# Two layers on one core: four instead of three groups of feed-forward columns by Strassen's product, second factors made in two portions, and another rule for the buffers of the condition sums

## The chip, the cores and the metric

The kernel runs on one core of a Trainium2 chip. The metric is the device time of one execution in microseconds (us). Three runs of the kernel before took 1845.4, 1853.11 and 1854.9, median 1853.11. The engines are named as in the profile: PE multiplies matrices (PEld is its loading of weights), DVE is VectorE, ACT is ScalarE, POOL is GpSimd, SP is SyncE; SP issues most loads.

## The reference

Two equal layers work on x of 512 tokens by 1024 features, in float32. A vector of conditions, `c_act = silu(c)`, gives six vectors of 1024 per layer:

```
mod = c_act @ w_ada + b_ada
shift1, scale1, gate1, shift2, scale2, gate2 = split(mod, 6)
h = rms_norm(x, norm1_g) * (1 + scale1) + shift1
...                                  # h @ w_in, three mixers (retention, gated linear, attention)
x = x + gate1 * (sum(gates * y_br) @ w_o)
h2 = rms_norm(x, norm2_g) * (1 + scale2) + shift2
u, g = split(h2 @ w_up, 2)           # 2 x 2816 columns
u = causal_dwconv(u, w_conv, b_conv) # three taps along the tokens
x = x + gate2 * ((silu(u) * g) @ w_down)
```

The change touches three places: the products `h2 @ w_up`, the sums `c_act @ w_ada` (the *condition sums*), and the pace at which the latter are put into the program.

## The kernel before, in words

Activations lie with features on the 128 partitions and the 512 tokens along the free dimension. A float32 product is made of three products of rounded parts (`mm3`, L320): high weight by high activation, high by low, low by high. All weights lie in DRAM as *units* of 128 x 1024 (512 KB), 338 of them, in the order of use. SP loads a unit into one of six raw buffers (`wr`, L180); ACT rounds it to its high part `wh` (L194); DVE takes `wl = wr - wh` (L203); then the raw buffer is free. A unit feeds 24 matmuls (8 blocks of 128 x 128, three products each). Weights are prepared some units ahead of their use: `depth` is how many units are rounded ahead, `far` how many more loads are issued.

The order of every engine's instructions is the order in which the Python program writes them; each engine goes through its own in order. `tick()` is called every few matmuls and puts in the next pieces of side work.

*Condition sums.* There are 80 blocks of `w_ada`, each 512 KB, which are summed beside the other work (another 32 half blocks are done at the start). One `ada_step` sums the block that was loaded in the step before (L230: a multiplication by `cact` and the sum along the free dimension) and then issues the next block's load (`ar`, L225) on SP. The block goes into one of the six raw buffers. `buffer()` takes the buffer that has been free longest, by `held`, which names for each the unit that used it last; the sum writes `held[ada_buf[0]] = -1`. A step is made in every second tick while `ada_on` is set, and in every tick while `ada_fast` is set. `ada_need(l, sec)` makes all steps up to a given sixth of the vector at once. Of the 80 sums, 34 stand in layer 0's merge and output product, 15 in its feed-forward product, 26 in its down product, and 5 in layer 1's merge.

*The feed-forward product* has 22 blocks of 128 columns for u and as many for g; a plain block takes two units (one of u, one of g), in 48 matmuls of 512 tokens, and `ff_evac` (L1072 and the lines before: scale, two taps, silu, product by g). The first three blocks stand with the normalization. Blocks 3 to J0 - 1 are plain, and the rest goes in groups of four by Strassen's product in Winograd's form: tokens are halved, the 1024 rows and the columns of a pair of blocks are halved, and 7 products replace 8. A group of four blocks takes 14 units where plain blocks take 8, with matmuls of 256 tokens (L1159, L1161, L1162). The combinations of the weights are made by loads that add to what is in the raw buffer (`accum_op`, on POOL's queue, L186, 8 per group). The combinations of the second factor, h2, are four sums per k (`ta`, `tb`; each holds two side by side) and their high and low parts (`tah`, `tal`, `tbh`, `tbl`), made once per layer for k = 0 to 3 and used by all groups: `t_sum` (5 DVE and 3 ACT operations) and `t_low` (3 DVE operations), one of these eight pieces after each of the first eight plain units. Within a group the evacuations are put at fixed units through `due`.

*The down product* has 8 blocks of 128 features over 22 k: the first three together, then one at a time; layer 0's last block is made by token halves, with the next layer's normalization behind it.

Of the kernel before, what the change touches and what calls it, by code (L numbers as in the profile page):

```python
# [50 lines left out]
NC = _o  # L51


NG = 3
J0 = KFF - 4 * NG
NI = 3
DN = [(j, k) for k in range(KFF) for j in range(NI)] + [(j, k) for j in range(NI, KD) for k in range(KFF)]
# [34 lines left out]
def tile_hybrid_layers(ctx: ExitStack, tc: tile.TileContext, xT, cvec, wall, wada, par, a2, cst, tabs, out):  # L92
# [23 lines left out]
    def free(n=1):  # L116
        live[0] -= n
# [108 lines left out]
            ada_raw.append((l, b, post, r))  # L226

    def ada_sum(l, b, r):
        held[ada_buf[0]] = -1
        V.scalar_tensor_tensor(out=r, in0=r, scalar=1.0, in1=cact, op0=ALU.mult, op1=ALU.mult,  # L230
                               accum_out=mod[l][:, b:b + 1])

# [59 lines left out]
    def tick(n=1, fl=True):  # L292
        for g in active:
            g[2] = False
        if cool[0] > 0:
            cool[0] -= 1
        if queue and len(active) < 8 and cool[0] == 0:
            it, cool[0] = queue.pop(0)
            active.append([it, next(it), False])
        advance("e")  # L300
        if fl:
            flush()
        advance("p")
        if ada_on[0] and (ada_fast[0] or tickcount[0] % 2 == 1):
            ada_step()
        tickcount[0] += 1
        if DBG:
            print("T", tickcount[0], len(active), len(queue), live[0], cur[0], [g[0].__name__ for g in active])
# [1 line left out]
    tickcount = [0]  # L310
    cool = [0]
    ada_on = [True]
    ada_fast = [False]

    def drain():
        flush()
# [249 lines left out]
    def layer(l, nm, h):  # L566
# [526 lines left out]

        tmid = {}

        def t_sum(k):
            ta, tb = slot("ta"), slot("tb")
            c, d = tks.pop((l, k)), tks.pop((l, k + 4))
            V.tensor_tensor(ta[:, H0], c[:, H0], c[:, H1], op=ALU.subtract)
            V.scalar_tensor_tensor(out=ta[:, H1], in0=d[:, H1], scalar=-1.0, in1=ta[:, H0], op0=ALU.mult,  # L1100
                                   op1=ALU.subtract)
            V.scalar_tensor_tensor(out=tb[:, H0], in0=d[:, H1], scalar=tabd[:, k:k + 1], in1=c[:, H1], op0=ALU.add,
                                   op1=ALU.subtract)
            V.tensor_tensor(tb[:, H1], d[:, H1], d[:, H0], op=ALU.subtract)
            V.tensor_tensor(tb[:, H1], tb[:, H1], ta[:, H0], op=ALU.add)
            ah, bh = slot("tah", F32R), slot("tbh", F32R)
            A.copy(ah[:, H0], ta[:, H0])
            A.activation(ah[:, H1], ta[:, H1], AF.Identity, bias=tabd[:, 4 + k:5 + k])
            A.copy(bh, tb)
            tmid[k] = ta, tb, ah, bh  # L1110

        def t_low(k):
            ta, tb, ah, bh = tmid.pop(k)
            al, bl = slot("tal", F32R), slot("tbl", F32R)
            V.tensor_tensor(al[:, H0], ta[:, H0], ah[:, H0].bitcast(F32), op=ALU.subtract)
            V.scalar_tensor_tensor(out=al[:, H1], in0=ta[:, H1], scalar=tabd[:, 4 + k:5 + k],
                                   in1=ah[:, H1].bitcast(F32), op0=ALU.add, op1=ALU.subtract)
            V.tensor_tensor(bl, tb, bh.bitcast(F32), op=ALU.subtract)
            tt[k, 1], tt[k, 2] = (ah, al, 0), (ah, al, 256)
            tt[k, 3], tt[k, 4] = (bh, bl, 0), (bh, bl, 256)  # L1120

        TS = [lambda: t_sum(0), lambda: t_low(0), lambda: t_sum(1), lambda: t_low(1),
              lambda: t_sum(2), lambda: t_low(2), lambda: t_sum(3), lambda: t_low(3)]

        def ff_group(j0):
            flush()
# [73 lines left out]
            def gate(t, i):  # L1200
                j = j0 + 2 * t + i
                V.tensor_tensor(act[j], act[j], gg[t][:, col(t, i)], op=ALU.mult)

            for t in range(2):
                at(1 + t, e1, t)
                at(3 + t, e5, t)
# [28 lines left out]
        ahead()  # L1235
        for j in range(3):
            pend.append(lambda j=j: ff_evac(j, fb[2 * j], fb[2 * j + 1]))
        free(NA)
        far[0] = 6
        for j in range(3, J0):  # L1240
            hold = {}

            def pu_evac(o, hold=hold):
                hold["u"] = o

            def pg_evac(o, hold=hold, j=j):
                ff_evac(j, hold["u"], o)

            col_block(h2, pu_evac)
            if TS:  # L1250
                TS.pop(0)()
            col_block(h2, pg_evac)
            if TS:
                TS.pop(0)()
        ada_on[0] = False
        far[0] = 12
        while ada_raw:
            i, b, post, r = ada_raw.pop(0)
            ada_sum(i, b, r)
            if post:  # L1260
                post()
        flush()
        for g in range(NG):
            ff_group(J0 + 4 * g)
# [33 lines left out]
                square_acc(j, acc3)  # L1298

        xl = list(range(KD))  # L1300
        act_to(4)
        far[0] = 4
        o2 = [bm() for _ in range(NI)]
        for kc in range(KFF):
# [9 lines left out]
                x[k] = slot("x")  # L1314
                Q.dma_start(out=x[k], in_=xm[l, k])
            if kc == 8:
                ada_on[0] = True
                ada_fast[0] = True
                far[0] = 1
            if kc % 2:  # L1320
                tick()
        ada_need(l, 5)
        for j in range(NI):
            pend.append(lambda j=j: dn_evac(j, o2[j]))
        for j in range(NI, KD if last else KD - 1):
            o = bm()
            for kc in range(KFF):
                wh, wl = wd(j, kc)
                mm3(o, wh, wl, acts[kc][0], acts[kc][1], kc == 0, kc == KFF - 1)
                if kc % 4 == 3:  # L1330
                    tick()

            pend.append(lambda j=j, o=o: dn_evac(j, o))
        flush()
        ada_fast[0] = False
        if last:
            return None, None
        ada_need(l + 1, 0)
# [218 lines left out]
```

## Time and profile before

| | |
|---|---|
| median of 3 runs | 1853.11 us |
| the profiled execution | 1846.68 us, span 1844.5 us |
| PE busy | 1784.8 us (97%) |
| DVE busy | 1085.7 us (59%) |
| ACT busy | 743.5 us (40%) |
| granted PE clock, mean | 0.985 |
| loaded from DRAM | 250.00 MB, 140 GB/s over the span |

The profile is one execution. A window of the trace (`A:B`, from the span's start) gives for each engine its busy time and the number of its instructions, then the granted PE clock, the share of time in which the load engines were busy, and the rate. A row of the timeline has start, duration, engine, line, operation, output <- inputs; in brackets stand the idle time before it and what ended that. A row of the waits has who waited for what: total us, how often, the longest. A costliest-groups row has count, busy us and mean ns, then the idle time just before. Lines are those of the kernel before. PE's matmuls overlap, so their pace is read from the distance of their starts, and a PE that is "busy" all the time may still run at half clock.

### The profile page before, as it was taken

Reading aid. Unit: us, or ns where it says so; the run is one execution under the profiler, and the core shown is the slowest. Engines: PE = TensorE matmul, PEld = TensorE weight load, DVE = VectorE, ACT = ScalarE, POOL = GpSimd, SP = SyncE. Lnnn points to the kernel's source line nnn. Section 1 sums busy time; section 2 is a strip of 40 time slices with the busy share of each in tenths; the row PEclk is TensorE's granted clock in tenths of the full one; section 3 lists DMA queues with packets and bytes.
Section 4 is the critical chain, followed back from the end, with each engine's and each line's share of the span. In section 5 each row is a group of like instructions: output and inputs, shape, how many; then the busy total and the mean of one; then the engine's idle time right before and its main releaser. Section 6 shows DMA issues by size and latency. Waiting matters only on the chain.

```text
span 1844.5 us, 24358 instructions
## 1 busy us (share of the span) xinstructions
PE 1784.8 (97%) x9601; PEld 1527.7 (83%) x9601; DVE 1085.7 (59%) x1639; ACT 743.5 (40%) x1233; POOL 147.7 (8%) x191
## 2 busy tenths in 40 slices
PE   8999999999899979999869999999999999999999
PEld 6888788888788869998668888788888898899887
DVE  7767654555566766685445667554434466566831
ACT  4664433422234335562115744333323234455520
POOL 3211100000010011100000101000000000111000
PEclk9999999999999989999979999999999999999999
DMA  9331232454462468854453322314242333488421
GB/s 359 126 130 58 74 99 83 146 181 177 168 223 97 161 184 215 212 200 166 177 194 110 108 92 69 104 69 149 92 147 93 122 108 92 121 210 217 160 99 50
DMA packets 78510, 259.99 MB, mean 141 GB/s; under 512 B 9096, under 2 KB 9522, under 8 KB 78396
## 3 DMA queue, kind: packets, MB, share of 16 engines
q1 hardware_dynamic: 68748, 224.86, 34.9%
q0 software_dynamic: 9648, 33.58, 8.6%
q8 instruction: 75, 1.23, 0.3%
q14 instruction: 39, 0.32, 0.0%
HBM read 250.00 MB, written 8.40 MB: 140 GB/s over the span
## 4 chain that ended last, share of the span: by engine, by line
PE 72%; DVE 12%; DMA 8%; ACT 4%; issue 3%; SPq 0%; POOL 0%; DVEq 0%; ACTq 0%; POOLq 0%
PE bm L321 13%; PE bm L322 13%; PE bm L323 13%; DMA ar<-wada 6%; PE bm L460 4%; PE ga L460 4%; PE bm L628 3%; PE bm L629 3%; PE bm L630 3%; PE bm L1159 3%; PE bm L1162 3%; PE bm L1161 3%; DMA wr<-wall 3%; DVE ar L230 2%; DVE wl L203 2%
## 5 line engine op out<-in xcount | busy, mean ns | idle before, releaser
L203 DVE TENSOR_TENSOR wl<-wr,wh 128x1024 fp32r<-128x1024 f32 x338 | 412.4, 1223 | 291.2 <-ACT wh L194 288.1
L194 ACT CAST wh<-wr 128x1024 fp32r<-128x1024 f32 x338 | 351.5, 1047 | 363.2 <-DMA wr<-wall 210.6
L321 PE MATMUL bm<-hhi,wh 128*128 128x512 f32 x912 | 366.1, 401 | 0.0
L323 PE MATMUL bm<-hhi,wl 128*128 128x512 f32 x912 | 355.7, 390 | 0.0
L322 PE MATMUL bm<-hlo,wh 128*128 128x512 f32 x912 | 355.5, 390 | 0.0
L321 PEld LDWEIGHTS bm<-hhi,wh 128*128 128x128 f32 x912 | 171.3, 188 | 37.1 <-issue 2.8
L323 PEld LDWEIGHTS bm<-hhi,wl 128*128 128x128 f32 x912 | 171.2, 188 | 37.1
L322 PEld LDWEIGHTS bm<-hlo,wh 128*128 128x128 f32 x912 | 171.5, 188 | 35.8 <-issue 1.4
L323 PE MATMUL bm<-fah,wl 128*128 128x512 f32 (+1 forms) x374 | 145.9, 390 | 17.2 <-DVE wl L203 17.2
L230 DVE SCALAR_TENSOR_TENSOR ar<-ar,cact 128x1024 f32<-128x1024 f32 x80 | 97.8, 1222 | 91.9 <-DMA ar<-wada 91.8
L321 PE MATMUL bm<-fah,wh 128*128 128x512 f32 (+1 forms) x374 | 145.7, 390 | 1.1 <-ACT wh L194 1.1
L322 PE MATMUL bm<-fal,wh 128*128 128x512 f32 (+1 forms) x374 | 144.9, 387 | 0.0
L323 PEld LDWEIGHTS bm<-fah,wl 128*128 128x128 f32 x374 | 74.5, 199 | 31.9 <-DVE wl L203 18.8
L628 PE MATMUL bm<-wh,hhi 128*128 128x512 f32 (+1 forms) x256 | 96.1, 376 | 0.0
L629 PE MATMUL bm<-wl,hhi 128*128 128x512 f32 (+1 forms) x256 | 93.5, 365 | 0.0
L630 PE MATMUL bm<-wh,hlo 128*128 128x512 f32 (+1 forms) x256 | 93.3, 365 | 0.0
L321 PEld LDWEIGHTS bm<-fah,wh 128*128 128x128 f32 x374 | 74.6, 200 | 14.3 <-ACT wh L194 1.4
L322 PEld LDWEIGHTS bm<-fal,wh 128*128 128x128 f32 x374 | 74.5, 199 | 13.1
L186 POOL DMA_DIRECT2D wr<-wall x48 | 41.7, 987 | 377.3 <-DVE wl L203 215.2
L321 PE MATMUL bm<-mxh,wh 128*128 128x256 f32 (+1 forms) x176 | 59.8, 340 | 8.0 <-ACT mxh L562 8.0
L322 PE MATMUL bm<-mxl,wh 128*128 128x256 f32 (+1 forms) x176 | 59.6, 338 | 0.0
L323 PE MATMUL bm<-mxh,wl 128*128 128x256 f32 (+1 forms) x176 | 59.1, 336 | 0.0
(288 smaller groups left out, 3368.5 us busy)
## 6 DMA issues: line engine op xcount, KB each, us to landing
wr<-wall SPq DMA_DIRECT2D x302, 512.0 KB, 4.3
ar<-wada SPq DMA_DIRECT2D x80, 512.0 KB, 3.5
wr<-wall POOLq DMA_DIRECT2D x48, 512.0 KB, 9.2
ad<-wada SPq DMA_DIRECT2D x32, 256.0 KB, 6.4
x<-xT SPq DMA_DIRECT2D x16, 256.0 KB, 4.5
x<-xm SPq DMA_DIRECT2D x16, 256.0 KB, 5.9
xm<-x POOLq DMA_DIRECT2D x10, 256.0 KB, 2.5
cumb<-cumd POOLq DMA_DIRECT2D x8, 256.0 KB, 4.8
```

Source lines behind the costliest of these rows:

```text
L194: A.copy(hi, raw[plan[i][1]])
L203: V.tensor_tensor(lo, raw[plan[i][1]], hi.bitcast(F32), op=ALU.subtract)
L230: V.scalar_tensor_tensor(out=r, in0=r, scalar=1.0, in1=cact, op0=ALU.mult, op1=ALU.mult, accum_out=mod[l][:, b:b + 1])
L321: T.matmul(o, lhsT=wh, rhs=ah, start=first, stop=False)
L322: T.matmul(o, lhsT=wh, rhs=al, start=False, stop=False)
L323: T.matmul(o, lhsT=wl, rhs=ah, start=False, stop=last)
L460: T.matmul(banks[f % GB][:, ts], lhsT=got[f // 8][wi][:, (f % 8) * 128:(f % 8) * 128 + 128], rhs=h[kc][hi][:, ts], start=kc == 0 and hf != ...
L628: T.matmul(o, lhsT=h[k][0][:, bs], rhs=wh[:, ws], start=k == 0, stop=False)
L629: T.matmul(o, lhsT=h[k][0][:, bs], rhs=wl[:, ws], start=False, stop=False)
L630: T.matmul(o, lhsT=h[k][1][:, bs], rhs=wh[:, ws], start=False, stop=k == KD - 1)
L1159: T.matmul(o, lhsT=wh[:, sl], rhs=ah, start=first and i == 0 and k == 0, stop=False, skip_group_check=True)
L1161: T.matmul(o, lhsT=wh[:, sl], rhs=al, start=False, stop=False, skip_group_check=True)
```

## The change

A group more per layer goes by Strassen's product: NG is 4, so J0 is 6; three plain blocks (6 units) remain behind the first three and 16 of the 22 blocks (56 units) are in groups. The second factor's combinations are cut into 16 pieces (`ta_sum`, `ta_low`, `tb_sum`, `tb_low` for k = 0 to 3). Twelve of them, the ta ones first, stand two after each of the six plain units; the other four (`TL`) stand in the first group, one at each of its units 1 to 4. The buffer of a condition sum is marked as freed by the newest unit (`state["lo"] - 1`), so it is taken last. The condition sums stop ahead of the plain blocks (the one that is still open is summed there) and start again when the first three down blocks are through, a step in every second tick; in the later down blocks a tick comes every three k, no longer every four. `ada_fast` goes. Of the 80 sums, 34 stand in layer 0's merge and output product as before, one ahead of its plain blocks, 13 in its down product and 32 in layer 1's merge and output product.

```diff
-NG = 3
+NG = 4
...
     def ada_sum(l, b, r):
-        held[ada_buf[0]] = -1
+        held[ada_buf[0]] = state["lo"] - 1
...
-        if ada_on[0] and (ada_fast[0] or tickcount[0] % 2 == 1):
+        if ada_on[0] and tickcount[0] % 2 == 1:
             ada_step()
...
-    ada_fast = [False]
...
-        def t_sum(k):
-            ta, tb = slot("ta"), slot("tb")
-            c, d = tks.pop((l, k)), tks.pop((l, k + 4))
+        def ta_sum(k):
+            ta, ah = slot("ta"), slot("tah", F32R)
+            c, d = tks[l, k], tks[l, k + 4]
             V.tensor_tensor(ta[:, H0], c[:, H0], c[:, H1], op=ALU.subtract)
             V.scalar_tensor_tensor(out=ta[:, H1], in0=d[:, H1], scalar=-1.0, in1=ta[:, H0], op0=ALU.mult,
                                    op1=ALU.subtract)
+            A.copy(ah[:, H0], ta[:, H0])
+            A.activation(ah[:, H1], ta[:, H1], AF.Identity, bias=tabd[:, 4 + k:5 + k])
+            tmid[k] = ta, ah
+
+        def ta_low(k):
+            ta, ah = tmid[k]
+            al = slot("tal", F32R)
+            V.tensor_tensor(al[:, H0], ta[:, H0], ah[:, H0].bitcast(F32), op=ALU.subtract)
+            V.scalar_tensor_tensor(out=al[:, H1], in0=ta[:, H1], scalar=tabd[:, 4 + k:5 + k],
+                                   in1=ah[:, H1].bitcast(F32), op0=ALU.add, op1=ALU.subtract)
+            tt[k, 1], tt[k, 2] = (ah, al, 0), (ah, al, 256)
+
+        def tb_sum(k):
+            tb, bh = slot("tb"), slot("tbh", F32R)
+            ta, _ = tmid[k]
+            c, d = tks.pop((l, k)), tks.pop((l, k + 4))
             V.scalar_tensor_tensor(out=tb[:, H0], in0=d[:, H1], scalar=tabd[:, k:k + 1], in1=c[:, H1], op0=ALU.add,
                                    op1=ALU.subtract)
             V.tensor_tensor(tb[:, H1], d[:, H1], d[:, H0], op=ALU.subtract)
             V.tensor_tensor(tb[:, H1], tb[:, H1], ta[:, H0], op=ALU.add)
-            ah, bh = slot("tah", F32R), slot("tbh", F32R)
-            A.copy(ah[:, H0], ta[:, H0])
-            A.activation(ah[:, H1], ta[:, H1], AF.Identity, bias=tabd[:, 4 + k:5 + k])
             A.copy(bh, tb)
-            tmid[k] = ta, tb, ah, bh
-
-        def t_low(k):
-            ta, tb, ah, bh = tmid.pop(k)
-            al, bl = slot("tal", F32R), slot("tbl", F32R)
-            V.tensor_tensor(al[:, H0], ta[:, H0], ah[:, H0].bitcast(F32), op=ALU.subtract)
-            V.scalar_tensor_tensor(out=al[:, H1], in0=ta[:, H1], scalar=tabd[:, 4 + k:5 + k],
-                                   in1=ah[:, H1].bitcast(F32), op0=ALU.add, op1=ALU.subtract)
+            tmid[k] = tb, bh
+
+        def tb_low(k):
+            tb, bh = tmid.pop(k)
+            bl = slot("tbl", F32R)
             V.tensor_tensor(bl, tb, bh.bitcast(F32), op=ALU.subtract)
-            tt[k, 1], tt[k, 2] = (ah, al, 0), (ah, al, 256)
             tt[k, 3], tt[k, 4] = (bh, bl, 0), (bh, bl, 256)
 
-        TS = [lambda: t_sum(0), lambda: t_low(0), lambda: t_sum(1), lambda: t_low(1),
-              lambda: t_sum(2), lambda: t_low(2), lambda: t_sum(3), lambda: t_low(3)]
+        TS = [lambda k=k, f=f: f(k) for k, f in ((0, ta_sum), (1, ta_sum), (0, ta_low), (2, ta_sum), (1, ta_low),
+                                                 (3, ta_sum), (2, ta_low), (0, tb_sum), (3, ta_low), (1, tb_sum),
+                                                 (0, tb_low), (2, tb_sum))]
+        TL = [lambda k=k, f=f: f(k) for k, f in ((1, tb_low), (3, tb_sum), (2, tb_low), (3, tb_low))]
...
+            for n in range(len(TL)):
+                at(1 + n, TL.pop(0))
             for t in range(2):
...
-        free(NA)
-        far[0] = 6
-        for j in range(3, J0):
-            hold = {}
-
-            def pu_evac(o, hold=hold):
-                hold["u"] = o
-
-            def pg_evac(o, hold=hold, j=j):
-                ff_evac(j, hold["u"], o)
-
-            col_block(h2, pu_evac)
-            if TS:
-                TS.pop(0)()
-            col_block(h2, pg_evac)
-            if TS:
-                TS.pop(0)()
         ada_on[0] = False
-        far[0] = 12
         while ada_raw:
             i, b, post, r = ada_raw.pop(0)
             ada_sum(i, b, r)
             if post:
                 post()
+        free(NA)
+        far[0] = 6
+        for j in range(3, J0):
+            hold = {}
+
+            def pu_evac(o, hold=hold):
+                hold["u"] = o
+
+            def pg_evac(o, hold=hold, j=j):
+                ff_evac(j, hold["u"], o)
+
+            col_block(h2, pu_evac)
+            for _ in range(2):
+                TS.pop(0)()
+            col_block(h2, pg_evac)
+            for _ in range(2):
+                TS.pop(0)()
+        far[0] = 12
         flush()
         for g in range(NG):
             ff_group(J0 + 4 * g)
...
         xl = list(range(KD))
+        ada_need(l, 5)
         act_to(4)
...
             if kc == 8:
-                ada_on[0] = True
-                ada_fast[0] = True
                 far[0] = 1
             if kc % 2:
                 tick()
-        ada_need(l, 5)
+        ada_on[0] = True
...
-                if kc % 4 == 3:
+                if kc % 3 == 2:
                     tick()
```

DVE in layer 0's down product, before: L230 is a condition sum, L203 a weight's low part, L1023 and L361 the evacuation of an output block.

```order
L203 TENSOR_TENSOR wl<-wr,wh 128x1024
L230 SCALAR_TENSOR_TENSOR ar,mod_88<-ar,cact 128x1024 x2
L203 TENSOR_TENSOR wl<-wr,wh 128x1024
L230 SCALAR_TENSOR_TENSOR ar,mod_88<-ar,cact 128x1024 x2
L203 TENSOR_TENSOR wl<-wr,wh 128x1024
L1023 SCALAR_TENSOR_TENSOR x<-bm,mod_87,x 128x512
L361 TENSOR_TENSOR acc<-acc,sq 128x512
L230 SCALAR_TENSOR_TENSOR ar,mod_88<-ar,cact 128x1024 x2
L203 TENSOR_TENSOR wl<-wr,wh 128x1024
```

The same place now; the evacuation's lines are L1022 and L360 in the new file.

```order
L203 TENSOR_TENSOR wl<-wr,wh 128x1024
L230 SCALAR_TENSOR_TENSOR ar,mod_88<-ar,cact 128x1024
L203 TENSOR_TENSOR wl<-wr,wh 128x1024
L230 SCALAR_TENSOR_TENSOR ar,mod_88<-ar,cact 128x1024 x2
L203 TENSOR_TENSOR wl<-wr,wh 128x1024
L1022 SCALAR_TENSOR_TENSOR x<-bm,mod_87,x 128x512
L360 TENSOR_TENSOR acc<-acc,sq 128x512
L230 SCALAR_TENSOR_TENSOR ar,mod_88<-ar,cact 128x1024
L203 TENSOR_TENSOR wl<-wr,wh 128x1024
L230 SCALAR_TENSOR_TENSOR ar,mod_88<-ar,cact 128x1024
```

Before, two sums stand between every weight and the next; now one and two in turn.

DVE at the start of layer 1's plain blocks, before: L1099 to L1105 are `t_sum`, L1115 to L1118 `t_low`, L1066 to L1078 a block's evacuation.

```order
L1099 TENSOR_TENSOR ta<-ht 128x256
L1100 SCALAR_TENSOR_TENSOR ta<-ht,ta 128x256
L1102 SCALAR_TENSOR_TENSOR tb<-ht,tabd 128x256
L1104 TENSOR_TENSOR tb<-ht 128x256
L1105 TENSOR_TENSOR tb<-tb,ta 128x256
L203 TENSOR_TENSOR wl<-wr,wh 128x1024
L1115 TENSOR_TENSOR tal<-ta,tah 128x256
L1116 SCALAR_TENSOR_TENSOR tal<-ta,tabd,tah 128x256
L1118 TENSOR_TENSOR tbl<-tb,tbh 128x512
L203 TENSOR_TENSOR wl<-wr,wh 128x1024
L1066 SCALAR_TENSOR_TENSOR fu<-bm,par_86,fu 128x511
L1068 SCALAR_TENSOR_TENSOR fu<-bm,par_86,fu 128x510
```

The same place now: L1098 and L1099 are `ta_sum`, L1108 and L1109 `ta_low`, L1065 to L1077 the evacuation.

```order
L1098 TENSOR_TENSOR ta<-ht 128x256
L1099 SCALAR_TENSOR_TENSOR ta<-ht,ta 128x256
L1098 TENSOR_TENSOR ta<-ht 128x256
L1099 SCALAR_TENSOR_TENSOR ta<-ht,ta 128x256
L203 TENSOR_TENSOR wl<-wr,wh 128x1024
L1108 TENSOR_TENSOR tal<-ta,tah 128x256
L1109 SCALAR_TENSOR_TENSOR tal<-ta,tabd,tah 128x256
L1098 TENSOR_TENSOR ta<-ht 128x256
L1099 SCALAR_TENSOR_TENSOR ta<-ht,ta 128x256
L203 TENSOR_TENSOR wl<-wr,wh 128x1024
L1065 SCALAR_TENSOR_TENSOR fu<-bm,par_86,fu 128x511
L1067 SCALAR_TENSOR_TENSOR fu<-bm,par_86,fu 128x510
```

The tb sums have moved behind all four ta sums. The weights' low parts keep their places, with two pieces between one and the next. The next rows of the same engine reach the low part that the first group's fourth unit uses (L203, the last row); L1117 to L1120 are `tb_sum`, L1127 is `tb_low`.

```order
L1117 SCALAR_TENSOR_TENSOR tb<-ht,tabd 128x256
L1119 TENSOR_TENSOR tb<-ht 128x256
L1120 TENSOR_TENSOR tb<-tb,ta 128x256
L203 TENSOR_TENSOR wl<-wr,wh 128x1024
L1127 TENSOR_TENSOR tbl<-tb,tbh 128x512
L1117 SCALAR_TENSOR_TENSOR tb<-ht,tabd 128x256
L1119 TENSOR_TENSOR tb<-ht 128x256
L1120 TENSOR_TENSOR tb<-tb,ta 128x256
L1065 SCALAR_TENSOR_TENSOR fu<-bm,par_86,fu 128x511
L1067 SCALAR_TENSOR_TENSOR fu<-bm,par_86,fu 128x510
L1077 TENSOR_TENSOR fu<-fu,bm 128x512
L203 TENSOR_TENSOR wl<-wr,wh 128x1024
```

Before, the last of the combinations stood behind the eighth of 14 plain units; now two `tb` sums and a `tb` low part stand within the two weights ahead of this one.

More of the change, by code (lines that the diff above doesn't have):

```diff
@@ L1237, in layer @@
             pend.append(lambda j=j: ff_evac(j, fb[2 * j], fb[2 * j + 1]))
+        ada_on[0] = False
+        while ada_raw:
+            i, b, post, r = ada_raw.pop(0)
+            ada_sum(i, b, r)
+            if post:
+                post()
         free(NA)
@@ L1249, in layer @@
             col_block(h2, pu_evac)
-            if TS:
+            for _ in range(2):
                 TS.pop(0)()
             col_block(h2, pg_evac)
-            if TS:
+            for _ in range(2):
                 TS.pop(0)()
-        ada_on[0] = False
         far[0] = 12
[L1257 to L1261, printed above, removed]
         flush()
@@ L1334, in layer @@
         flush()
-        ada_fast[0] = False
         if last:
```

## The prediction

> **What bounds the kernel now.** I read the busy shares first, then the chain that ended last.
>
> ```profile
> PE 1784.8 (97%) x9601; PEld 1527.7 (83%) x9601; DVE 1085.7 (59%) x1639; ACT 743.5 (40%) x1233; POOL 147.7 (8%) x191
> PE 72%; DVE 12%; DMA 8%; ACT 4%; issue 3%; SPq 0%; POOL 0%; DVEq 0%; ACTq 0%; POOLq 0%
> ```
>
> PE is nearly always at work, but the chain runs through it for only 72% of the time; for 20% the end was set by VectorE and by loads. To see where, I cut the span into stages that exist in both layers, with the same matmuls in each, and put the layers beside each other.
>
> ```profile
> core 0: us, PE busy (x) PEld busy (x) DVE busy (x) ACT busy (x) POOL busy (x), PEclk, DMA share, GB/s
> 62.82:589.34 526.52, 516.41 (x2652) 431.27 (x2651) 318.30 (x504) 213.86 (x407) 39.19 (x42) 0.99 0.38 132
> 1009.30:1523.34 514.04, 511.91 (x2650) 429.41 (x2649) 281.36 (x437) 207.34 (x397) 38.97 (x42) 1.00 0.31 104
> 589.34:665.50 76.16, 76.16 (x338) 63.06 (x336) 55.88 (x91) 29.38 (x41) 1.84 (x2) 1.00 0.49 159
> 1523.34:1599.49 76.15, 76.15 (x337) 63.06 (x336) 48.97 (x74) 33.44 (x47) 2.65 (x3) 1.00 0.33 94
> 665.50:805.11 139.61, 125.70 (x1010) 124.63 (x1008) 92.20 (x109) 72.61 (x94) 19.15 (x22) 0.95 0.78 200
> 1599.49:1720.45 120.96, 120.96 (x1010) 120.95 (x1008) 81.42 (x92) 68.92 (x89) 18.06 (x21) 1.00 0.81 205
> 805.11:963.33 158.22, 134.15 (x605) 113.43 (x603) 85.59 (x125) 39.11 (x54) 5.10 (x9) 0.90 0.52 186
> 1720.45:1840.15 119.70, 119.70 (x530) 98.92 (x528) 45.62 (x54) 31.59 (x42) 0.00 (x0) 1.00 0.27 95
> ```
>
> In pairs, layer 0 then layer 1: projections with merge and output product; the 14 plain feed-forward units; the 42 Strassen units; the down product. Layer 1's PE never waits after the merge (busy equals length, granted clock 1.00). Layer 0 is 12.5, 0, 18.65 and 38.5 us longer. What layer 0 has and layer 1 nearly lacks is the condition sums (75 of their 80). Their rows:
>
> ```profile
> L230 DVE SCALAR_TENSOR_TENSOR ar<-ar,cact 128x1024 f32<-128x1024 f32 x80 | 97.8, 1222 | 91.9 <-DMA ar<-wada 91.8
> ar<-wada SPq DMA_DIRECT2D x80, 512.0 KB, 3.5
> SPq L225 <- DVE ar L230: 402.5, 66, 24.8
> 859.77 1.23 DVE L230 SCALAR_TENSOR_TENSOR ar<-ar,cact 128x1024 f32<-128x1024 f32 x1 [2.14 <-DMA ar<-wada]
> 864.55 1.23 DVE L230 SCALAR_TENSOR_TENSOR ar<-ar,cact 128x1024 f32<-128x1024 f32 x1 [3.55 <-DMA ar<-wada]
> ```
>
> The sums' work is small (97.8 us); their wait for their own loads is as long (91.8 us). The third row is the sync queue: 66 of the loads waited for the sum before, 402.5 us in all, and in that time the weight loads queued behind them did not start. The reason is `held[...] = -1`: the buffer just summed counts as the one free longest, so the next load goes into it and can't start before the sum. One step is then load 3.5 plus sum 1.2, about 4.8 us (859.77 to 864.55), in VectorE's order. In the down product a step comes every four matmul triples once the first three columns are done. A matmul's spacing there:
>
> ```profile
> 1589.97 0.39 PE L321 MATMUL bm<-hhi,wh 128*128 128x512 f32 x1
> 1590.20 0.39 PE L322 MATMUL bm<-hlo,wh 128*128 128x512 f32 x1
> ```
>
> 0.227 us (finer over a whole unit: 76.15 / 14 = 5.44 per unit of 24), so four triples are 2.7 us against a step of 4.8: PE waits for VectorE.
>
> **The change, part by part.** The sum goes against the profiled execution's 1846.7 us (span 1844.5 and 2.2 around it); the median of the runs is 1853.1.
>
> *Condition sums in layer 0's down product: -36.* The stage is 158.22 against 119.70; 2.5 of that stays, by my estimate: layer 0's last column is made by halves (for the output product's last column, which is cut alike, that costs 18.15 in place of 3 x 5.44 = 16.3) and it carries the next layer's squares.
>
> ```profile
> 536.48:554.63 18.15, 18.15 (x154) 18.15 (x152) 9.18 (x21) 4.72 (x10) 3.71 (x7) 1.00 0.66 238
> ```
>
> So 36.0 is stall. After the change 13 sums run here in place of 26, one every six triples (4.1 us), and each load goes to a buffer freed four to seven VectorE operations ago, by the order, so it starts early. If it were serial all the same, 13 steps would each lose 4.8 - 4.1 = 0.7, some 10 us: the term lies between -26 and -36. I take -36, since 13 sums with 22 units are 35 loads of 0.52 MB in 122 us, 150 GB/s, and the Strassen stage moves 205 without a wait.
>
> *Layer 0's Strassen stage: -18.65.* Its first wait stands at its head:
>
> ```profile
> 684.87 0.58 PE L1159 MATMUL ba<-tah,wh 128*128 128x256 f32 x1 [9.14 <-ACT wh L194]
> ```
>
> Weights were late because SP's queue stood behind condition loads up to the stage's head, and one of the six buffers was theirs. Now the sums are off before the plain blocks, so all six serve weights. What is late next there is the second term below.
>
> *Layer 0's merge: -12.5* (526.52 - 514.04). Most of it is one wait:
>
> ```profile
> 509.11 0.79 PE L321 MATMUL bm<-mxh,wh 128*128 128x512 f32 x1 [7.27 <-ACT mxh L562]
> ```
>
> The same 34 sums stay in this stage; only their waiting goes. VectorE's 318.30 of 526.52 us leaves room for them.
>
> *Layer 1's merge gets 32 sums in place of 5: 0.* They are 27 x 1.22 = 33 us on a VectorE busy 281.36 of 514.04, and bring the stage to layer 0's load of 318. The end to the bad is the 12.5 that layer 0 loses with the same sums and the old buffer rule.
>
> *A fourth group by Strassen's product in each layer: -6.4.* Eight plain units become 14 units of 256-wide matmuls:
>
> ```profile
> 1649.89 0.28 PE L1159 MATMUL ba<-tah,wh 128*128 128x256 f32 x1
> 1650.01 0.28 PE L1161 MATMUL ba<-tal,wh 128*128 128x256 f32 x1
> ```
>
> A unit is 120.96 / 42 = 2.88, a group 14 x 2.88 = 40.3 against 8 x 5.44 = 43.5: -3.2 per layer. The Trainium skill, "TensorE: Matmul & The Clock Gate", section "Back-to-back issue gap", speaks against the change: it gives a stream of matmuls about 81 ns apart at width 128 and 131 ns at 512. Interpolated to 98 at 256 (an estimate from that page), a group would be 24 x 14 x 0.098 = 32.9 against 24 x 8 x 0.131 = 25.2, a loss of 7.7 per layer. The rows differ from it, 227 and 120 ns, and they decide; here the 256-wide matmul costs 0.53 of the 512-wide.
>
> *The second-factor sums before the first group: +14.* This is the cost. Six plain units, not 14, now cover the making of the combinations. VectorE's cycle per pair of plain units, layer 1, from the timeline:
>
> ```profile
> 1533.32 0.42 DVE L1099 TENSOR_TENSOR ta<-ht 128x256 f32<-128x256 f32 x1
> 1533.77 0.42 DVE L1100 SCALAR_TENSOR_TENSOR ta<-ht,ta 128x256 f32<-128x256 f32 x1
> 1534.11 0.48 DVE L1102 SCALAR_TENSOR_TENSOR tb<-ht,tabd 128x256 f32<-128x256 f32 x1
> 1534.51 0.42 DVE L1104 TENSOR_TENSOR tb<-ht 128x256 f32<-128x256 f32 x1
> 1534.96 0.42 DVE L1105 TENSOR_TENSOR tb<-tb,ta 128x256 f32<-128x256 f32 x1
> 1537.02 1.23 DVE L203 TENSOR_TENSOR wl<-wr,wh 128x1024 fp32r<-128x1024 f32 x1 [1.64 <-ACT wh L194]
> 1538.17 0.42 DVE L1115 TENSOR_TENSOR tal<-ta,tah 128x256 fp32r<-128x256 f32 x1
> 1538.50 0.48 DVE L1116 SCALAR_TENSOR_TENSOR tal<-ta,tabd,tah 128x256 fp32r<-128x256 f32 x1
> 1538.90 0.68 DVE L1118 TENSOR_TENSOR tbl<-tb,tbh 128x512 fp32r<-128x512 f32 x1
> 1539.50 1.22 DVE L203 TENSOR_TENSOR wl<-wr,wh 128x1024 fp32r<-128x1024 f32 x1
> 1540.63 0.74 DVE L1066 SCALAR_TENSOR_TENSOR fu<-bm,par,fu 128x511 f32<-128x511 f32 x1
> ...
> 1543.52 0.42 DVE L1099 TENSOR_TENSOR ta<-ht 128x256 f32<-128x256 f32 x1
> ```
>
> By starts, a ta sum is 0.8, a ta low part 0.73, a tb sum 1.27, a tb low part 0.6, a weight's low part 1.14, a block's evacuation 2.9. In the new order VectorE stands at the same place at 1533.3, and up to and with the low part for the group's fourth unit it has 4 x 0.8 + 4 x 0.73 + 3 x 1.27 + 0.6 = 10.5 of pieces, 6 x 1.14 = 6.8, 3 x 2.9 = 8.7, and 6 waits of the kind of 1537.02's, 1.64 each, 9.8: 35.8, until 1569.1. PE gets there at 1523.34 + 6 x 5.44 + 3 x 2.88 = 1564.6. It waits 4.5. What comes after a wait of that length:
>
> ```profile
> 896.54 0.80 PE L323 MATMUL bm<-fah,wl 128*128 128x512 f32 x1 [3.75 <-DVE wl L203]
> 898.41 0.63 PE L321 MATMUL bm<-fah,wh 128*128 128x512 f32 x1
> 898.84 0.63 PE L322 MATMUL bm<-fal,wh 128*128 128x512 f32 x1
> ```
>
> Spacing 0.43, half the speed; over as long as the wait itself that is about 2 more. With a little for the rest of the group's pieces, 7 per layer. Without the waits on ACT VectorE would be ahead, and the term 0; with 3.2 more (the last four pieces all before that unit) it is 10. Both layers alike, since the sums are off.
>
> Accumulating loads on the POOL queue cost nothing beyond their issue, in layer 1 without a PE wait; the moved `ada_need` calls find nothing left to do.
>
> Sum: 1846.7 - 36.0 - 18.65 - 12.5 - 6.4 + 14 = 1787. The profiled execution lay 6.4 below the median; the step chain that can vary is largely gone, so I add half: **1790 us**.
>
> **The rivals.** *No new wait:* VectorE keeps ahead of the first group; for it, layer 1 has no wait in its first group now; against it, 8 units of cover less. 1790 - 14 = 1776.
>
> *First group as bad as layer 0's today:* 18.65 in each layer in place of 7, by VectorE's lag and the accumulating loads behind it: 1790 + 23 = 1813. For it, the same place waited 9.14 at once when VectorE had 55.88 of work in the plain stage, against 48.97; against it, that wait had condition loads ahead in the queue.
>
> *Loads still waited for:* the buffer rule moves the wait to another load, layer 0's merge keeps its 12.5 and layer 1's gets the same: 1815. Against it, the order shows every one of these loads behind an operation at least four back.
>
> *Slower: every Strassen group waits.* Eight groups of loads that must accumulate, on engines busy 0.81 of the stage already; if each loses what layer 0's stage lost, 8 x 18.65 = 149 in place of 14: 1925. It decides from 11 us a group (1776 + 8 x 11 = 1864). Against it, layer 1's 120.96 has no idle time in three groups running.
>
> *The page's rule:* 256-wide matmuls cost more than half. As a mechanism, a group would lose 7.7 in place of winning 3.2: 1790 + 2 x 10.9 = 1812. The spacing rows say no.
>
> **How the numbers follow.** Forecast 0.63, no new wait 0.07, bad first group 0.13, loads still waited for 0.09, every group waiting 0.07, the page's rule 0.01. The forecast's own range is 1776 (no wait) to 1806 (wait of 10, down at -26). The range of 1775 to 1816 reaches over the first group's and the loads' rivals, and leaves out every group waiting and the cases in which two of them add up. This kernel's runs tell 0.5% from no change, 9 us: faster means below 1844, slower above 1862. All cases but every group waiting end below 1844: 0.93; of its 0.07, 0.03 fall about the old time (9 us a group) and 0.04 above.
>
> **What would show it.** Layer 0's down stage near 122 with hardly a wait of L230 on its load; SP's wait of L225 on L230 gone from the list; both merges 514; 6 plain and 56 Strassen units taking 6 x 5.44 + 56 x 2.88 = 194 and about 7, so 201 in both layers; a PE idle gap of 3 to 6 us near the first group's fourth unit, released by VectorE's low part. A merge of 526 in layer 1, a gap over 10 at the first group, or gaps in groups two to four would show me wrong.

## The result, and the profile after

The changed kernel takes 1807.78 us (median of four runs, 1800.83 to 1810.11) against 1852.37 before (four runs): a ratio of 0.9759, 95% interval 0.9721 to 0.9797. It is faster, inside the range, and 18 us above the forecast of 1790. The profiled execution took 1808.5 us, so no correction from it to the median is due. Two rows of the changed kernel's page, its busy times and the condition sums:

```profile
PE 1769.9 (98%) x9889; PEld 1530.0 (85%) x9889; DVE 1104.8 (61%) x1663; ACT 760.3 (42%) x1261; POOL 161.3 (9%) x207
L230 DVE SCALAR_TENSOR_TENSOR ar<-ar,cact 128x1024 f32<-128x1024 f32 x80 | 97.2, 1218 | 0.0
```

PE is busy for 98% of a shorter span, though with waits inside. The second row is the plainest success: VectorE's 80 condition sums take as long as before and now wait for nothing (91.8 us before). Their loads still wait in SP's queue for an earlier sum, though a fifth as long as before (402.5 us, 66 times):

```profile
SPq L225 <- DVE ar L230: 82.7, 20, 10.6
```

The forecast had this row gone from the list; that sign failed, without a cost that the stages show.

The stages, layer 0 then layer 1 of each pair: merge, plain units (now 6), Strassen units (now 56), down product.

```profile
core 0: us, PE busy (x) PEld busy (x) DVE busy (x) ACT busy (x) POOL busy (x), PEclk, DMA share, GB/s
63.11:577.97 514.86, 512.77 (x2652) 429.88 (x2652) 319.41 (x506) 212.95 (x407) 40.97 (x44) 1.00 0.42 136
956.49:1470.46 513.97, 511.92 (x2649) 429.46 (x2648) 312.31 (x495) 206.90 (x397) 40.74 (x44) 1.00 0.41 133
577.97:610.61 32.64, 32.64 (x146) 27.03 (x145) 21.20 (x35) 14.94 (x23) 0.00 (x0) 1.00 0.29 84
1470.46:1503.10 32.64, 32.64 (x145) 27.04 (x144) 21.21 (x35) 14.93 (x23) 0.00 (x0) 1.00 0.22 63
610.61:789.04 178.43, 167.43 (x1345) 165.81 (x1344) 119.42 (x143) 96.65 (x127) 26.11 (x30) 0.97 0.77 188
1503.10:1682.74 179.64, 167.31 (x1346) 165.39 (x1345) 119.50 (x143) 96.27 (x127) 25.77 (x30) 0.97 0.76 187
789.04:910.50 121.46, 121.46 (x604) 103.43 (x603) 69.71 (x98) 38.84 (x54) 5.09 (x9) 1.00 0.53 187
1682.74:1802.61 119.87, 119.86 (x530) 98.92 (x528) 45.61 (x54) 31.56 (x42) 0.00 (x0) 1.00 0.28 96
```

Both merges are at 514, layer 1's too, although it now makes 32 sums; layer 0's down product is at 121.46. Only one stage is off: 56 Strassen units at 2.88 are 161.3, and they take 178.4 and 179.6, 17 and 18 us more, in both layers. The forecast had 7 in each. That stage in layer 1, group by group (14 units each):

```profile
1503.10:1553.92 50.82, 43.58 (x337) 42.67 (x336) 31.27 (x41) 24.00 (x32) 6.87 (x8) 0.93 0.69 166
1553.92:1596.56 42.64, 40.84 (x339) 40.44 (x338) 28.14 (x33) 22.94 (x31) 6.87 (x8) 1.00 0.80 198
1596.56:1640.56 44.00, 42.07 (x339) 41.87 (x338) 29.84 (x35) 24.37 (x32) 6.87 (x8) 0.96 0.78 192
1640.56:1682.74 42.18, 40.82 (x339) 40.42 (x338) 30.26 (x37) 24.95 (x35) 5.17 (x6) 1.00 0.78 196
```

The first group loses 10.5 against 40.3, the other three 2.3, 3.7 and 1.9. What PE waits for, from its timeline in the same stage:

```profile
1515.15 0.58 PE L1169 MATMUL ba<-tah,wh 128*128 128x256 f32 x1 [3.25 <-ACT wh L194]
1516.41 0.58 PE L1172 MATMUL ba<-tah,wl 128*128 128x256 f32 x1 [0.46 <-DVE wl L203]
1535.63 0.38 PE L1169 MATMUL bm<-tbh,wh 128*128 128x256 f32 x1 [2.87 <-ACT uu L1186]
1578.27 0.39 PE L1169 MATMUL bm<-tbh,wh 128*128 128x256 f32 x1 [1.15 <-ACT uu L1186]
1621.69 0.39 PE L1169 MATMUL bm<-tbh,wh 128*128 128x256 f32 x1 [1.93 <-ACT uu L1186]
```

The first two rows are the wait that was forecast, at the first group's fourth unit. The other three are another kind: at the ninth unit of every group PE wants to add to a bank of PSUM (the memory that matrix products are summed in) that ScalarE has not yet copied out (`uu`, L1186). ScalarE's timeline around the second of them:

```profile
1570.30 1.05 ACT L194 CAST wh<-wr 128x1024 fp32r<-128x1024 f32 x1 [3.94 <-DMA wr<-wall]
1574.15 1.05 ACT L194 CAST wh<-wr 128x1024 fp32r<-128x1024 f32 x1 [2.80 <-DMA wr<-wall]
1576.69 1.05 ACT L194 CAST wh<-wr 128x1024 fp32r<-128x1024 f32 x1 [1.49 <-DMA wr<-wall]
1577.64 0.58 ACT L1186 COPY uu<-bm 128x512 f32<-128x512 f32 x1
1580.47 1.05 ACT L194 CAST wh<-wr 128x1024 fp32r<-128x1024 f32 x1 [2.26 <-DMA wr<-wall]
1581.43 0.58 ACT L1186 COPY uu<-bm 128x512 f32<-128x512 f32 x1
```

The copy that PE waits for stands in ScalarE's order behind the rounding of weights some units ahead, and the rounding waits for a load. In the waits of the two kernels' layer 1 stages, after first, then before:

```profile
ACT wh L194 <- DMA wr<-wall: 62.7, 26, 5.5
PE bm L1169 <- ACT uu L1186: 8.6, 7, 2.9
ACT tbh L1121 <- DVE tb L1120: 7.6, 3, 3.1
```

```profile
ACT wh L194 <- DMA wr<-wall: 19.9, 11, 2.7
```

The roundings waited for loads before as well, but never so long that PE felt it there. (The row of `tbh` is ScalarE waiting for VectorE's tb sums in the first group, with the roundings of weights queued behind it.)

### The profile page after: what moved, and what is told of

The parts are those of the page before. It is cut to its first block, busy times and chain, and to the rows that moved or that the text cites. A ratio compares the mean times of both kernels' runs of the same rounds, so it can differ in the third digit from the quotient of the medians.

```text
span 1806.7 us, 24956 instructions
## 1 busy us (share of the span) xinstructions
PE 1769.9 (98%) x9889; PEld 1530.0 (85%) x9889; DVE 1104.8 (61%) x1663; ACT 760.3 (42%) x1261; POOL 161.3 (9%) x207
## 4 chain that ended last, share of the span: by engine, by line
PE 70%; issue 10%; DVE 8%; DMA 8%; ACT 4%; POOL 0%; SPq 0%; POOLq 0%; ACTq 0%; DVEq 0%
PE bm L320 15%; PE bm L322 15%; PE bm L321 15%; DMA wr<-wall 7%; PE bm L459 3%; PE bm L627 3%; PE bm L628 3%; PE bm L629 3%; PE ga L459 3%; DVE wl L203 2%; ACT wh L194 2%; PE bm L1169 1%; PE bm L1172 1%; PE bm L1171 1%; DVE fl L751 1%
## 5 line engine op out<-in xcount | busy, mean ns | idle before, releaser
L203 DVE TENSOR_TENSOR wl<-wr,wh 128x1024 fp32r<-128x1024 f32 x350 | 426.9, 1223 | 299.6 <-ACT wh L194 298.7
L320 PE MATMUL bm<-hhi,wh 128*128 128x512 f32 x784 | 316.3, 403 | 0.0
L322 PE MATMUL bm<-hhi,wl 128*128 128x512 f32 x784 | 306.0, 390 | 0.0
L321 PE MATMUL bm<-hlo,wh 128*128 128x512 f32 x784 | 305.7, 390 | 0.0
L320 PEld LDWEIGHTS bm<-hhi,wh 128*128 128x128 f32 x784 | 147.3, 188 | 31.9 <-issue 2.8
L322 PEld LDWEIGHTS bm<-hhi,wl 128*128 128x128 f32 x784 | 147.2, 188 | 32.0
L321 PEld LDWEIGHTS bm<-hlo,wh 128*128 128x128 f32 x784 | 147.4, 188 | 31.0 <-issue 1.4
L230 DVE SCALAR_TENSOR_TENSOR ar<-ar,cact 128x1024 f32<-128x1024 f32 x80 | 97.2, 1218 | 0.0
L1169 PE MATMUL bm<-tbh,wh 128*128 128x256 f32 x256 | 75.2, 294 | 15.6 <-ACT uu L1186 15.6
L186 POOL DMA_DIRECT2D wr<-wall x64 | 55.5, 980 | 372.9 <-DVE wl L203 255.6
L1022 DVE SCALAR_TENSOR_TENSOR x<-bm,mod,x 128x512 f32<-128x512 f32 (+1 forms) x39 | 25.3, 654 | 79.7 <-PE bm L322 76.3
L1172 PE MATMUL bm<-tbh,wl 128*128 128x256 f32 x256 | 73.8, 288 | 0.0
```

The source lines that it names most:

```text
L203: V.tensor_tensor(lo, raw[plan[i][1]], hi.bitcast(F32), op=ALU.subtract)
L320: T.matmul(o, lhsT=wh, rhs=ah, start=first, stop=False)
L321: T.matmul(o, lhsT=wh, rhs=al, start=False, stop=False)
L322: T.matmul(o, lhsT=wl, rhs=ah, start=False, stop=last)
L1169: T.matmul(o, lhsT=wh[:, sl], rhs=ah, start=first and i == 0 and k == 0, stop=False, skip_group_check=True)
L1172: T.matmul(o, lhsT=wl[:, sl], rhs=ah, start=False, stop=k == 3, skip_group_check=True)
```

## The experiments

The theory after these lines (A): VectorE's combination pieces make the weights of the first group late; the accumulating loads, which must wait for VectorE to let go of the buffer, start late with them; that lateness reaches ScalarE's roundings in every later group and, by ScalarE's order, the copies and PE. Rivals: six plain units are too short to load ahead, whatever VectorE does (B); a group's loop of loads and accumulations is itself slower than PE (C). Times are medians of four executions, with the ratio to runs of the kernel before that were made beside them; where there was one execution, the text says so.

**Without the combinations.**

```diff
...
 def ta_sum(k):
-    (the sums, and their high part)
+    pass
 def ta_low(k):
-    (two subtractions; tah and tal as the high and low parts)
+    tt[k, 1], tt[k, 2] = (*h2[k], 0), (*h2[k], 256)
...
 def tb_low(k):
-    (one subtraction; tbh and tbl)
+    tt[k, 3], tt[k, 4] = (*h2[k + 4], 0), (*h2[k + 4], 256)
```

> The changed kernel without the making of the second factor's combinations (the products take parts of h2 in their place, so VectorE and ScalarE lose that work and the output is not the reference's). Theory A, late start: the pieces delay the weights' low parts in the six plain units, the accumulating loads wait for those, and the lateness stays through all four groups. Then the 56 Strassen units take 161 us in both layers (now 178.4 and 179.6), PE waits for no copy of uu, and the time is 1808 - 35 = 1773. Theory B, loads: six plain units are too short to load ahead whatever VectorE does. Then only the wait at the fourth unit goes, 6.5 per layer, the groups stay at 42 to 44 us each, and the time is 1795.

Measured: 1782.21 us, ratio 0.9602 (0.9574 to 0.9631); Strassen stages 163.5 and 166.3. Layer 1's first and last group:

```profile
1488.08:1528.39 40.31, 40.31 (x337) 40.31 (x336) 24.81 (x27) 20.61 (x25) 6.58 (x8) 1.00 0.79 196
...
1610.03:1654.39 44.36, 42.06 (x338) 41.86 (x337) 31.94 (x39) 26.33 (x37) 5.17 (x6) 0.96 0.75 189
```

The first groups run without a wait, so B falls for them: six units are enough to load ahead for a group if VectorE keeps up. But the fourth group waits after all (2.2 and 4.0, and 1.0 in layer 1's third), and the total is 9 above A's. Without the pieces the lead lasts for two or three groups, not for four, and ScalarE's roundings in layer 1's stage still wait long for loads:

```profile
ACT wh L194 <- DMA wr<-wall: 45.6, 21, 5.8
```

So VectorE's pieces make only a part of that lateness (62.7 with them). Whether the rest is C, or what six plain units leave of the lead, this run does not tell.

**Three groups, the rest of the change kept.**

```diff
-NG = 4
+NG = 3
...
-            for _ in range(2):
-                TS.pop(0)()
+                for _ in range(2 if TS else 1):
+                    if TS or TL:
+                        (TS or TL).pop(0)()
```

> The changed kernel with three groups per layer (14 plain units ahead of them; all 16 pieces stand there, two after each of the first six units, one after each of the next four), the condition sums as in the change. A and B: both lateness and shortage of load time are gone, 42 Strassen units take 121 in both layers, the time is 1808 - 35.4 + 6.4 = 1779. Theory C, the loop of loads and accumulations in a group is itself slower than PE: each of the six groups keeps about 2.3, so 1793.

Measured: 1782.8 us, ratio 0.9612 (0.959 to 0.9633). Both layers' 42 units:

```profile
653.86:774.81 120.95, 120.95 (x1009) 120.95 (x1008) 81.60 (x92) 69.12 (x89) 18.29 (x21) 1.00 0.81 205
1532.36:1653.31 120.95, 120.95 (x1009) 120.95 (x1008) 81.41 (x92) 68.91 (x89) 18.07 (x21) 1.00 0.81 205
```

No wait at all. So the fourth group, which should have won 6.4, costs 25 (1807.8 - 1782.8) as the change makes it; the change's whole gain and more is in the condition sums. A loop that is slower than PE from the first group on (C as it was put) falls as well.

**Evacuations ahead of the preparation.** The lines only change places.

```diff
-                    prep_lo(cur[0] + 3)
-                    prep_hi(cur[0] + 4)
-                    dma_to(cur[0] + 12, True)
                     for f in due.pop(cur[0], []):
                         f()
+                    prep_lo(cur[0] + 3)
+                    prep_hi(cur[0] + 4)
+                    dma_to(cur[0] + 12, True)
```

> The changed kernel, with a unit's evacuations written ahead of the preparation of the units to come (before, ScalarE's copy of uu stands behind the rounding of a unit whose load is late). If ScalarE's order makes PE wait, the 8 us per layer in groups two to four and the 4 at the first group's ninth unit go, about 1808 - 24 = 1784. If the loads set the pace, PE waits for weights in place of copies, and the time stays at 1808 within 5.

Measured: 1790.88 us, ratio 0.9657 (0.9639 to 0.9675), 17 below the changed kernel where 24 was expected. Layer 1's first and second group; the third and fourth read as the second:

```profile
1496.51:1543.50 46.99, 43.01 (x337) 42.51 (x336) 33.14 (x44) 23.49 (x31) 6.87 (x8) 0.93 0.74 179
1543.50:1583.82 40.32, 40.32 (x338) 40.32 (x337) 28.94 (x34) 24.07 (x32) 6.87 (x8) 1.00 0.87 210
...
```

PE's waits for the copies did not turn into waits for weights. The roundings still wait 39.8 us for loads in layer 1's stage, and PE no longer feels it: it was ScalarE's order that handed a late load on to PE. In layer 0, 1.9 us stay in groups two to four. The first group keeps 6.7 (7.2 in layer 0): the fourth unit's wait.

**The tb pieces inside the first group.** All eight at its units 0 to 7; the plain units keep the eight ta pieces.

```diff
-  (TS: eight ta pieces and four tb pieces; TL: four tb pieces)
+  (TS: the eight ta pieces; TL: the eight tb pieces)
...
             for n in range(len(TL)):
-                at(1 + n, TL.pop(0))
+                at(n, TL.pop(0))
...
-  (two pieces after each plain unit)
+  (two pieces after each of the first two plain units, then one)
```

> The changed kernel with all eight tb pieces at the first group's units 0 to 7 and only the eight ta pieces in the six plain units (two after each of the first two, then one). Theory A, late start by VectorE's pieces: 5 us of VectorE work leave the plain units, the wait at the first group's fourth unit (6.5 per layer) goes and the first group ends near 43; groups two to four keep under 2 each: 1808 - 18 = 1790. If the pieces in the group are as bad as ahead of it, the first group stays at 50 and the time at 1808.

Measured: 1792.65 us, ratio 0.9679 (0.9655 to 0.9704). The stages, layer 0 and layer 1:

```profile
611.02:787.33 176.31, 166.76 (x1345) 165.54 (x1344) 117.68 (x142) 94.95 (x125) 25.54 (x30) 0.97 0.77 191
1501.38:1672.98 171.60, 164.55 (x1345) 163.12 (x1344) 117.59 (x142) 95.19 (x125) 25.20 (x30) 0.99 0.78 196
```

The first groups come to 42.2 and 42.7, and the fourth unit's wait is gone. Groups two to four do not keep under 2 each as I had expected, but 1.5 to 6.4: as long as ScalarE's order stays, their waits for copies stay. (The profiled execution, 1798.75 us, is the slowest of the four.)

**Both edits.** The diffs of the last two runs in one kernel:

```diff
-                    prep_lo(cur[0] + 3)
...
                         f()
+                    prep_lo(cur[0] + 3)
...
-                at(1 + n, TL.pop(0))
+                at(n, TL.pop(0))
```

> Both edits: evacuations ahead of the preparation and the tb pieces in the first group. If the two causes add up, 56 Strassen units take 161 to 164 in each layer, 1773 to 1779, faster than any kernel so far. If they are one and the same wait, no better than the better one of the two alone, 1790.

Measured: 1774.33 us (1773.4 to 1778.2), ratio 0.9583 (0.9562 to 0.9605). The 56 units, layer 0 and layer 1:

```profile
609.46:771.18 161.72, 161.52 (x1345) 161.31 (x1344) 117.22 (x141) 93.61 (x124) 25.53 (x30) 1.00 0.83 205
1485.22:1647.61 162.39, 161.53 (x1345) 161.32 (x1344) 117.58 (x141) 93.41 (x124) 25.21 (x30) 1.00 0.83 204
```

By the medians the two causes add up (17 and 15 alone, 33 together). The loads are not on time here either; the roundings in layer 1's stage still wait 52.9 us, where the changed kernel's wait 62.7, while PE loses 1.1:

```profile
ACT wh L194 <- DMA wr<-wall: 52.9, 22, 5.0
```

This is the fastest kernel of the study, 33 below the changed one: its fourth group now brings its gain, 6.0 against the three-group kernel by the spans of the two profiles (1777.6 and 1771.6), 8.5 by the medians (of runs on two chips), where 6.4 was worked out.

**Without the accumulating loads** (the weights' combinations are left out).

```diff
             _, dst, src, _ = accs.pop(0)
-            G.dma_start(out=raw[dst], in_=wall[src], accum_op=ALU.add)
```

> The changed kernel without the 8 accumulating loads of a group (the weights' combinations are left out, so the output is not the reference's). If groups two to four wait because those loads land about 10 us after VectorE has let go of the buffer, they come to 40.3 each in both layers and the first keeps only the wait at its fourth unit, 45 to 47: 56 units in 167. If VectorE's lag alone makes the waits, the stage stays near 178.

Measured: 1786.77 us (one execution). Layer 1's first and second group, with the third and fourth like the second:

```profile
1493.42:1539.74 46.32, 42.31 (x337) 41.90 (x336) 34.46 (x46) 25.22 (x33) 0.00 (x0) 0.96 0.29 92
1539.74:1580.06 40.32, 40.32 (x338) 40.32 (x337) 28.26 (x33) 23.41 (x31) 0.00 (x0) 1.00 0.32 105
...
```

The stage is 168.1 and 167.3: 6.8 and 6.0 of wait are left in each layer, all in the first group. That is the part that the pieces make by themselves; the other 10 and 12 come through the accumulating loads. With them went a good part of the load traffic (a DMA share of 0.29 to 0.41 in place of 0.69 to 0.80), so the run does not tell their latency from their traffic. How long they take from issue to landing stands in the changed kernel's profile beside the plain ones (KB each, median us):

```profile
wr<-wall SPq DMA_DIRECT2D x302, 512.0 KB, 3.6
ar<-wada SPq DMA_DIRECT2D x80, 512.0 KB, 4.3
wr<-wall POOLq DMA_DIRECT2D x64, 512.0 KB, 9.4
```

A buffer that is added to again four units later, after 4 x 2.88 = 11.5 us, needs 9.4 for the load and 1.05 and 1.22 for the rounding and the low part: 11.7, an estimate from medians, and no slack. That fits with a lead that, once lost, is not won back inside the groups. It is not shown to make a wait by itself: the median is 9.3 in the three-group kernel and 9.9 in the one with both edits, which hardly wait, and the single loads of the changed kernel lie between 5.3 and 14.0. An earlier issue is not open to the load, since the low part must first have read what the buffer holds; the trace has that wait, `POOL wr L186 <- DVE wl L203`, 117.3 us in 13 times in layer 1's stage. The Trainium skill, "DMA: Bandwidth & Descriptors", section "Rules for kernel authors", gives a reason to wait for earlier transfers too: an accumulating transfer reads its destination and writes it later with nothing held in between, so that another transfer's write that lands in between is lost. No run here shows that.

**The condition sums alone.** First the kernel before with the new buffer rule and nothing else.

```diff
     def ada_sum(l, b, r):
-        held[ada_buf[0]] = -1
+        held[ada_buf[0]] = state["lo"] - 1
```

> The kernel before with only the new rule for the buffer of a condition sum. If the serial load and sum was all that the condition sums cost, the 12.5 of the merge, the 18.65 of layer 0's Strassen stage and most of the down product's 36 go: 1853 - 67 = 1786 to 1796. If the pace of the steps costs as well (26 sums in the down product, one every 2.7 us, and a buffer less for weights at the first group), the merge's 12.5 goes and half or less of the rest: 1815 to 1840.

Measured: 1801.07 us, ratio 0.9722 (0.9688 to 0.9757). Layer 0's merge, Strassen stage and down product:

```profile
61.74:576.53 514.79, 512.70 (x2652) 430.12 (x2651) 318.26 (x504) 212.88 (x407) 39.14 (x42) 1.00 0.39 135
653.36:794.60 141.24, 126.68 (x1009) 124.93 (x1008) 92.10 (x109) 72.09 (x94) 19.14 (x22) 0.96 0.77 200
794.60:916.05 121.45, 121.45 (x604) 103.47 (x603) 84.64 (x125) 38.83 (x54) 5.09 (x9) 1.00 0.68 242
```

The time lies between the two that were expected: one line gives the merge and the whole of the down product, with all of its sums at the old pace, and nothing of the Strassen stage. So the slower pace in the down product, and the later start, were not needed. The Strassen stage's 20 us have another cause.

Then the kernel before with the sums stopped ahead of the plain blocks and nothing else:

```diff
+        ada_on[0] = False
+        while ada_raw:
+            (the open sum is made here)
         free(NA)
         far[0] = 6
         for j in range(3, J0):
...
-        ada_on[0] = False
```

> The kernel before with the condition sums stopped ahead of the plain blocks, nothing else (the old buffer rule, three groups). If layer 0's 18.65 in the Strassen stage comes from the condition loads in the queue and the buffer that they hold, the stage falls to 121 and the merge keeps its 12.5 and the down product its 36 or more (the sums not made go there or to layer 1's merge): 1828 to 1840. If it comes from the combinations' pieces, it stays at 139.

Measured: 1831.7 us (one execution). The same three stages:

```profile
63.03:590.12 527.09, 516.63 (x2652) 431.45 (x2651) 319.26 (x506) 213.62 (x407) 39.12 (x42) 0.99 0.37 129
666.28:789.63 123.35, 121.45 (x1009) 121.04 (x1008) 81.21 (x92) 68.99 (x89) 18.28 (x21) 1.00 0.80 200
789.63:947.64 158.01, 134.31 (x604) 112.95 (x603) 85.44 (x125) 39.12 (x54) 5.09 (x9) 0.90 0.53 186
```

The mirror image: the Strassen stage is repaired but for 2.4 and the other two keep their waits. The two edits are separate gains.

What of the sums in the plain blocks made the stage late? Two variants of the three-group kernel, one execution each, take them apart: a buffer withheld without any load, and VectorE's work without load and buffer.

```diff
         far[0] = 6
+        hb = buffer(1 << 30)
...
+        held[hb] = state["lo"] - 1
         far[0] = 12
```

> The three-group kernel (e2) with one of the six raw buffers kept from the weights through the 14 plain units of each layer, as a condition load kept it before; no condition loads or sums there. If the buffer is what layer 0's Strassen stage lacked, the first group takes 54 to 59 in both layers and the time is 1815 to 1820. If it was the queue or VectorE's sums, all groups stay at 40.3 and the time at 1783.

Measured: 1782.5 us, first and second groups at 40.3 in both layers, third ones at 42.8 and 41.2. The buffer alone is not it; it costs 2.5 and 0.8, by the wait for a copy at the third group's ninth unit.

```diff
...
+        if dm and tickcount[0] % 2 == 1:
+            for i in range(2):
+                V.scalar_tensor_tensor(out=dm[0], in0=cact[:, hs], ..., accum_out=dm[1][:, i:i + 1])
...
```

> The three-group kernel (e2) with 14 sums of the same size in the plain units of each layer, made of data that is always there: VectorE's work of the condition sums without their loads and without their buffer. If VectorE's work made layer 0's stage late, the first group takes 50 or more in both layers, 1805 and up. If the loads or the buffer did, the groups stay at 40.3, 1783.

Measured: 1803.02 us. Layer 0's plain stage and first group:

```profile
578.16:659.71 81.55, 78.63 (x337) 63.96 (x336) 61.34 (x119) 29.80 (x43) 1.84 (x2) 0.98 0.31 91
659.71:705.96 46.25, 41.99 (x338) 41.69 (x337) 30.65 (x39) 23.37 (x29) 7.42 (x9) 0.96 0.75 183
```

11.3 us are lost in layer 0 (5.4 and 5.9 against 76.16 and 40.3) and 11.8 in layer 1; the first groups take 46.3 and 47.8, neither the expected 40.3 nor 50. VectorE's work alone is enough to make the stage late, by something over half of the 20. It is no exact copy. Each sum is made in two halves, which take 1.54 us with the reading of their totals where a sum takes 1.30. And 5.4 are lost in the plain units, where the kernel before lost nothing with its sums (76.16) and the one with the new buffer rule 0.7 (76.83). What the loads beside the sums add stays open.

## Why the prediction was right or wrong

**Condition sums in the down product, -36:** right; 158.22 became 121.46, -36.8. The mechanism was the one named, a load into the buffer just summed. The pace counted for nothing: all 26 sums at the old pace gave 121.45.

**Layer 0's merge, -12.5:** -11.7, right, and by the buffer rule alone. **Layer 1's merge, 0:** 514.04 became 513.97, right; the rival "loads still waited for" falls.

**Layer 0's Strassen stage, -18.65:** the size is right (the three-group kernel has 120.95) and the cause partly wrong. I named the condition loads in SP's queue and the buffer they held. The buffer alone costs nothing in the first group, and a stand-in for VectorE's work, without loads, costs 11; the share of the loads stays open.

**A fourth group, -6.4:** PE's part is right, 2.88 for a 256-wide unit wherever PE does not wait. The forecast's estimate of 98 ns at that width, worked out from the Trainium skill, "TensorE: Matmul & The Clock Gate", section "Back-to-back issue gap", would have made a group cost more; the 6 gained by the kernel with both edits speak against it.

**The new wait, +14:** this term failed; it measured 17.1 + 18.3 = 35.4, and the missing 21.4 are the whole of the error (1787 + 21.4 = 1808, the profiled execution's 1808.5). That the time still lies in the range is due to the room left for other rivals, not to this term; gaps in groups two to four, which the forecast had named as a sign against it, came. The wait at the fourth unit itself was right: forecast 7 in a layer, 6.8 and 6.0 measured without the accumulating loads. ScalarE's high part ended it rather than VectorE's low part, and behind that stands the same work: ScalarE rounds the `tb` pieces ahead of that weight and waits for VectorE's sums of them (7.6 us in the row of `tbh`).

The step that failed is the sentence that accumulating loads "cost nothing beyond their issue, in layer 1 without a PE wait". They cost nothing behind 14 plain units, there and again in the three-group kernel. Behind six the lead is shorter: even without the pieces the fourth group loses 2.2 and 4.0. With the pieces VectorE is late as well, the loads start later, and in all four groups ScalarE's order turns late loads into waits of PE for a copy; without the accumulating loads, or with the copies ahead, groups two to four lose nothing or nearly nothing. That the loop of additions has no slack is an estimate, and how the remaining lateness divides between it and the six units stays open. I had looked at which waits PE had before, and not at how far those engines were from making it wait.

**The 3 us** added for the median were not there: 1807.78 against 1808.5.

## What to carry to other kernels

A buffer that was just used is the worst one to load into if its free time is written as "longest ago": one line of bookkeeping made 49 us of waits here (11.7 in the merge and 36.8 in the down product). A stage without a PE wait may still live on a lead won earlier; before shortening the stage ahead of it, compare the time between a buffer's release and its next use with the time its load takes. In an engine that goes in order, put what another engine waits for ahead of work that waits for a load.

## What the runs showed of the hardware

After PE's wait of 3.25 us at 1515.15 the matmuls started 0.21 us apart until 1520.84, in place of 0.12; the mean granted clock of that whole group was 0.93. By the starts of the units the one that holds the wait took 6.29 and the one behind it 5.94 in place of 2.88 each: the wait and what came after it cost 6.5, near twice its length. In the kernel with both edits the Strassen stages run at a DMA share of 0.83 and about 205 GB/s with 0.4 and 1.1 us lost. In the kernel before with only the new buffer rule, layer 0's down product takes in 242 GB/s, all 26 sums among it, with no wait of PE.
